# A feed-forward in seven block products instead of eight, in an encoder layer on one core

## The chip, the core and the metric

The kernel runs on one core of a Trainium2 chip. Five engines work side by side, each through its own instructions in order: TensorE (PE in the profile, its weight loads PEld), VectorE (DVE), ScalarE (ACT), GpSimd (POOL) and SyncE (SP, which issues the transfers here). Data lie in device memory, in SBUF (128 partitions) and in PSUM (eight banks of 128 x 512 floats, into which TensorE adds up). The metric is the device time of one execution in microseconds (us), the median of the runs.

## The reference

One layer of a hybrid encoder is applied to two request groups of 512 tokens, with the same weights, in float32. With D = 1024 and a feed-forward width of 2816, cut to what matters here:

```python
h = rmsnorm(x, g_mix)
u = h @ w_in                      # feeds an mLSTM, an attention and merge gates
...
x = x + (g_m * y_m + g_a * y_a) @ w_out     # y_m = (sigmoid(o) * hm) @ w_mo, y_a = attention @ w_ao

h2 = rmsnorm(x, g_ffn)
x = x + (silu(h2 @ w_gate) * (h2 @ w_up)) @ w_down

x = x + sigmoid(x @ w_ple_gate) * (p_l @ w_ple)
return rmsnorm(x, g_final)        # after the only layer
```

## The kernel before, in words

**Tiles.** Activations are held transposed: a tile has 128 features on the partitions and the 512 tokens of one group along the row. So `x` is eight tiles per group (`KD` = 8), and the feed-forward's inner activations are 22 (`NF`). The two groups are `g` = 0 and 1.

**Precision.** Every operand of a product is split into a high part (`hi`, type fp32r, a cast on ACT) and the rest (`lo`, a subtraction on DVE, `lo_of`). A product is three matmuls: hi by hi, hi by lo and lo by hi. `proj1` does that for one column block of 128 outputs: for each of eight slices of the contraction three matmuls into one bank, 24 in all.

**Weights.** `weight(src)` loads a column block of a weight (128 x 1024) into a staging tile `wst`, makes `whi` on ACT and `wlo` on DVE; `w8(name)` picks the block from a table. There are two buffers of each, so the next block's weights are made while TensorE works. Each block serves both groups: 48 matmuls.

**Order of the stages.** Input and first norm; gates and four mLSTM heads with their projections; attention over eight heads with merge gates between; then the part that the change touches: the mLSTM's output projection (`mo`, with values `z1` kept in SBUF), the attention's (`ao`, which makes `y`), the output projection (`out`, which adds the residual into `x2`), the feed-forward, the embedding stage, and the final norm of each group.

**Feed-forward before.** The operands `h2` are `x2` times the gain `g_ffn`, split, without the rows' norm: they are made while the output projection still runs. The norm `rs2` of each group is applied to the products afterwards. The 22 inner column blocks come in three parts (`FF_PARTS` = 8, 8, 6). In a part, for each inner block the gate product is scaled by the norm, put through Silu and scaled again, then multiplied with the up product, and split; then eight `w_down` blocks (`wd0` to `wd2`) are multiplied with the part's activations and added to `x2`.

**Embedding stage before.** `x2` is split again (`x3`). For each of eight column blocks and both groups there are a gate product (`pg`, 24 matmuls) and a product of the embedding's projection (`emb`: `wple` by `pp`, six matmuls), then `embed` on ACT and DVE. The second group's last four blocks come after the first group's, whose final norm is computed meanwhile; its last two blocks run in halves of 256 tokens.

**What sets the order.** A planner orders each engine's instructions when the kernel is built: it takes the written order as priority, gives out buffer slots as they come free, and places the waits. Two stages can thus mix on an engine. A pool of tiles (`Slots`) gives each tag a fixed number of slots; pools opened after others are closed reuse their memory, and their tiles wait for the old ones that they overlap.

Of the kernel before, what the change touches and what calls it, by code (L numbers as in the profile page):

```python
# [62 lines left out]
def encoder_kernel(ctx: ExitStack, tc: tile.TileContext, a):  # L63
# [3 lines left out]
    cp = ctx.enter_context(tc.tile_pool(name="const", bufs=1))  # L67
    wp = ctx.enter_context(tc.tile_pool(name="wp", bufs=1))
    sm = ctx.enter_context(tc.tile_pool(name="sm", bufs=1))
# [4 lines left out]
    def nm(s):  # L74
        ids[0] += 1
        return f"{s}_{ids[0]}"

    class Slots:
# [8 lines left out]
        def close(self):  # L87
            self.ctx.close()

    EV = Slots("EV", ch=2, bk=2)  # L90

# [50 lines left out]
    def weight(src):  # L142
        n = src.shape[-1]
        st = wp.tile([P, 1024], F32, name=nm("wst"), tag="wst", bufs=WB[0])
        nc.sync.dma_start(st[:, :n], src)
        hi = wp.tile([P, 1024], F32R, name=nm("whi"), tag="whi", bufs=WB[1])
        S.copy(hi[:, :n], st[:, :n])  # L147
        lo = wp.tile([P, 1024], F32R, name=nm("wlo"), tag="wlo", bufs=WB[2])
        lo_of(lo[:, :n], st[:, :n], hi[:, :n])
        return hi, lo  # L150
# [12 lines left out]
    def w8(name):  # L163
        return weight(a["w8"][W8[name]])
# [82 lines left out]

    # ---- input, scaled by the first gain; its rows' norms are applied to the products
    LAT = Slots("LAT", raw=8)
# [49 lines left out]

    # ---- gate rows, compressed q and kv  # L300
    gsd = [dr.tile([64, T], F32, name=f"gsd{g}") for g in range(G)]
# [16 lines left out]

    # ---- gates
    nmr = MC.pool.tile([P, T], F32R, name="nmr")  # L320
# [102 lines left out]

    # ---- mLSTM heads
    R.close()
# [146 lines left out]

    # ---- norms of the compressed q and kv, on top of their rows' first norm
    def lat_norms():
# [186 lines left out]
    z1 = [[None] * KD for _ in range(G)]  # L761
# [14 lines left out]
    for c in range(KD):  # L776
        w = w8(f"ao{c}")
        for g in range(G):
            bk = proj1(w, ox[g])
            t = load(tad[g][c])  # L780
            V.scalar_tensor_tensor(out=t, in0=t, scalar=1.0, in1=bk, op0=ALU.add, op1=ALU.mult)
            V.tensor_tensor(out=t, in0=t, in1=z1[g][c], op=ALU.add)
# [4 lines left out]
            y[g][c] = (hi, lo)  # L787

    # ---- output projection, residual, second norm
    x2 = [[None] * KD for _ in range(G)]  # L790
    h2 = [[None] * KD for _ in range(G)]
    ss = [SumSq(L, "tr") for _ in range(G)]
    for c in range(KD):
        w = w8(f"out{c}")
        for g in range(G):
            bk = proj1(w, y[g])
            x = load(a[f"x{g}"][c], QL, "lat", "x2")
            V.tensor_tensor(out=x, in0=x, in1=bk, op=ALU.add)
            x2[g][c] = x
            ss[g].add(x)  # L800
            h2[g][c] = gsplit(x, col("g_ffn", c), L, "B", "h2")
    rs2 = []
    for g in range(G):
        t = H("rs", "rs2")
        S.copy(t, ss[g].rstd_bank(D))
        rs2.append(t)

    # ---- feed-forward
    f0 = 0
    for pi, nf in enumerate(FF_PARTS):  # L810
        act = [[], []]
        for f in range(f0, f0 + nf):
            w = w8(f"fg{f}")
            sg = []
            for g in range(G):
                s = L("tr", "sg")
                V.tensor_tensor(out=s, in0=rs2[g], in1=proj1(w, h2[g]), op=ALU.mult)  # L817
                S.activation(out=s, in_=s, func=AF.Silu)
                V.tensor_tensor(out=s, in0=s, in1=rs2[g], op=ALU.mult)
                sg.append(s)  # L820
            w = w8(f"fu{f}")
            for g in range(G):
                V.tensor_tensor(out=sg[g], in0=sg[g], in1=proj1(w, h2[g]), op=ALU.mult)  # L823
                act[g].append(split(sg[g], H, "h", "ac"))
        for c in range(KD):
            w = weight(a[f"wd{pi}"][c])
            for g in range(G):
                V.tensor_tensor(out=x2[g][c], in0=x2[g][c], in1=proj1(w, act[g], nf), op=ALU.add)  # L828
        f0 += nf

    # ---- per-layer embedding; the second group ends after the first, which is normed meanwhile
    def final_norm(g, b0=0, nb=NB, pool=(2, 5)):
        tok, n = slice(b0 * P, (b0 + nb) * P), nb * P
        bc = ss[g].rstd_bank(D, b0, nb)
        rf = H("rs", "rsf")[:, tok]
        S.copy(rf, bc)
        per = T // n
        for c0 in range(0, KD, per):
            ob = H("h", "o")
            for i in range(per):  # L840
                c = c0 + i
                o, x = ob[:, i * n : (i + 1) * n], x2[g][c][:, tok]
                if c in pool:
                    S.activation(out=o, in_=x, func=AF.Copy, scale=col("g_final", c))
                    GP.tensor_tensor(out=o, in0=o, in1=rf, op=ALU.mult)
# [7 lines left out]
    pp = [[split(load(a[f"p{g}"][k]), H, "h", "pl") for k in range(2)] for g in range(G)]  # L853
    x3 = [[None] * KD for _ in range(G)]
    for c in range(KD):
        for g in range(G):
            x3[g][c] = split(x2[g][c], L, "B", "x3")
    wple = []
    for i in range(2):
        st = wp.tile([P, 1024], F32, name=nm("wst"), tag="wst", bufs=WB[0])  # L860
        nc.sync.dma_start(st, a["wple"][i])
        for j in range(2):
            wple.append(split(st[:, j * T : (j + 1) * T], H, "h", "we"))
    ss = [SumSq(L, "tr") for _ in range(G)]

    def embed(c, g, bp, bk, tok=slice(0, T)):
        t, x = EV("ch", "pt")[:, tok], x2[g][c][:, tok]
        S.activation(out=t, in_=bk, func=AF.Tanh, scale=0.5)
        V.scalar_tensor_tensor(out=t, in0=t, scalar=1.0, in1=bp, op0=ALU.add, op1=ALU.mult)
# [3 lines left out]
    def emb(c, g, tok=slice(0, T)):  # L873
        return proj1(wple[c // 2], pp[g], 2, (c % 2) * 256, tok=tok)

    lead = KD - LAG
    for c in range(lead):
        w = w8(f"pg{c}")
        bks = [proj1(w, x3[g]) for g in range(G)]
        for g in range(G):  # L880
            embed(c, g, emb(c, g), bks[g])
    for c in range(lead, KD):
        bk = proj1(w8(f"pg{c}"), x3[0])
        embed(c, 0, emb(c, 0), bk)
    ws = [w8(f"pg{c}") for c in range(lead, lead + 2)]
    final_norm(0)
    for c in range(lead, KD - 2):
        bk = proj1(ws.pop(0), x3[1])
        ws.append(w8(f"pg{c + 2}"))
        embed(c, 1, emb(c, 1), bk)  # L890
    for b0, nb in ((0, NB // 2), (NB // 2, NB // 2)):
        tok = slice(b0 * P, (b0 + nb) * P)
        for c in range(KD - 2, KD):
            bp = emb(c, 1, tok)
            embed(c, 1, bp, proj1(ws[c - KD + 2], x3[1], tok=tok), tok)
        final_norm(1, b0, nb, (2, 5) if b0 else range(KD))
    L.close()
    QL.close()
    H.close()
    LAT.close()  # L900
    EV.close()
    banks(None, None)


WB = (2, 2, 2)
LAG = 4
# [95 lines left out]
```

## Time and profile before

| | |
|---|---|
| median of 3 runs | 2009.96 us (2009.62 to 2010.03) |
| span of the profiled execution, first to last instruction | 2009.2 us; no other time is listed for that execution |
| mean granted TensorE clock | 0.994 |
| busy in the span | PE 1980.5, DVE 983.7, ACT 691.7, POOL 67.7 us |
| transfers | 140.93 MB, mean 70 GB/s |

Busy time of PE counts overlapping matmuls once in the totals; a single matmul's duration is longer than the distance to the next one, so the rate is read from how many start in a window. The wait lists say which engine waited for which; an entry under SPq is a transfer that waits in SyncE's queue before it is issued. POOL's spans are rough.

### The profile page before, as it was taken

To read this page: it belongs to the slowest core of one execution; us is meant where nothing else is said; L and a number is where in the kernel's file an instruction comes from. 1 tells how busy PE (TensorE), PEld (TensorE's weight loads), DVE (VectorE), ACT (ScalarE), POOL (GpSimd) and SP (SyncE) were. 2 spreads that over 40 slices of the span, in tenths; PEclk is the share of its full clock that TensorE was granted. 3 is DMA by queue.
4 is the path that set the end of the run, shared out by engine and by line. 5 is a ranking of instruction groups with operands and counts; after the bars stand their busy time and mean duration, and the time that the engine had idled before them with its cause. 6 is when DMAs were issued, how large, how long until landed. Compare 5 with 4: busy or idle time off the path is not lost.

```text
span 2009.2 us, 23492 instructions
## 1 busy us (share of the span) xinstructions
PE 1980.5 (99%) x9318; PEld 1627.7 (81%) x9318; DVE 983.7 (49%) x1799; ACT 691.7 (34%) x1303; POOL 67.7 (3%) x88
## 2 busy tenths in 40 slices
PE   7999999999999999999999999999999999999996
PEld 6788898988888787888888888888888888888886
DVE  6747575745554767843444533322333222334436
ACT  5345455525344657841122321211121101212223
POOL 3000000000000000000000000000000000000002
PEclk9999999999999999999999999999999999999998
DMA  4110101111341212532431111111111111111212
GB/s 155 48 43 32 64 33 53 38 68 69 118 155 66 90 44 91 190 130 74 137 126 53 43 43 52 43 53 42 53 43 53 42 53 42 53 35 61 74 53 95
DMA packets 62734, 140.93 MB, mean 70 GB/s; under 512 B 6752, under 2 KB 17376, under 8 KB 62624
## 3 DMA queue, kind: packets, MB, share of 16 engines
q1 hardware_dynamic: 62624, 139.43, 20.0%
q8 instruction: 73, 1.20, 0.2%
q14 instruction: 37, 0.30, 0.0%
HBM read 113.88 MB, written 25.53 MB: 69 GB/s over the span
## 4 chain that ended last, share of the span: by engine, by line
PE 97%; DVE 2%; ACT 1%; issue 0%; DMA 0%; DVEq 0%; SPq 0%; ACTq 0%
PE mm L160 26%; PE mm L158 26%; PE mm L159 26%; PE nm L546 3%; PE mm L464 2%; PE mm L463 2%; PE mm L465 2%; PE pt L722 1%; PE pj L158 1%; PE pj L159 1%; PE pj L160 1%; PE sc L705 1%; PE av L729 1%; PE av L731 1%; PE av L730 1%; PE sc L709 1%
## 5 line engine op out<-in xcount | busy, mean ns | idle before, releaser
L147 ACT CAST whi<-wst 128x1024 fp32r<-128x1024 f32 (+1 forms) x159 | 163.9, 1031 | 556.7 <-PE mm L159 500.5
L160 PE MATMUL mm<-h2h,wlo 128*128 128x512 f32 x704 | 279.2, 397 | 0.0
L158 PE MATMUL mm<-h2h,whi 128*128 128x512 f32 x704 | 279.1, 396 | 0.0
L159 PE MATMUL mm<-h2l,whi 128*128 128x512 f32 x704 | 279.1, 396 | 0.0
L158 PE MATMUL mm<-hh,whi 128*128 128x512 f32 x592 | 237.1, 401 | 7.0 <-ACT whi L147 6.8
L160 PE MATMUL mm<-hh,wlo 128*128 128x512 f32 x592 | 236.2, 401 | 2.3 <-DVE wlo L133 2.2
L159 PE MATMUL mm<-hl,whi 128*128 128x512 f32 x592 | 237.0, 401 | 1.1 <-DVE hl L245 1.1
L133 DVE TENSOR_TENSOR wlo<-wst,whi 128x1024 fp32r<-128x1024 f32 (+1 forms) x159 | 191.6, 1205 | 90.1 <-ACT whi L147 89.6
L159 PEld LDWEIGHTS mm<-h2l,whi 128*128 128x128 f32 x704 | 132.6, 188 | 32.3
L160 PEld LDWEIGHTS mm<-h2h,wlo 128*128 128x128 f32 x704 | 132.6, 188 | 32.3
L158 PEld LDWEIGHTS mm<-h2h,whi 128*128 128x128 f32 x704 | 132.6, 188 | 32.2
L158 PEld LDWEIGHTS mm<-hh,whi 128*128 128x128 f32 x592 | 113.0, 191 | 33.4 <-ACT whi L147 6.8
L160 PE MATMUL mm<-ach,wlo 128*128 128x512 f32 x352 | 139.6, 396 | 0.0
L159 PE MATMUL mm<-acl,whi 128*128 128x512 f32 x352 | 139.6, 396 | 0.0
L158 PE MATMUL mm<-ach,whi 128*128 128x512 f32 x352 | 139.5, 396 | 0.0
L160 PEld LDWEIGHTS mm<-hh,wlo 128*128 128x128 f32 x592 | 112.6, 190 | 29.2 <-DVE wlo L133 3.4
L159 PEld LDWEIGHTS mm<-hl,whi 128*128 128x128 f32 x592 | 112.8, 191 | 28.6 <-DVE hl L245 2.3
L828 DVE TENSOR_TENSOR x<-x,mm 128x512 f32<-128x512 f32 x48 | 33.0, 687 | 159.9 <-PE mm L160 159.9
L823 DVE TENSOR_TENSOR sg<-sg,mm 128x512 f32<-128x512 f32 x44 | 30.2, 688 | 140.2 <-PE mm L160 140.2
L817 DVE TENSOR_TENSOR sg<-rs,mm 128x512 f32<-128x512 f32 x44 | 30.3, 688 | 138.3 <-PE mm L160 136.6
L158 PEld LDWEIGHTS mm<-ach,whi 128*128 128x128 f32 x352 | 66.3, 188 | 16.2
L159 PEld LDWEIGHTS mm<-acl,whi 128*128 128x128 f32 x352 | 66.3, 188 | 16.2
(289 smaller groups left out, 3700.5 us busy)
## 6 DMA issues: line engine op xcount, KB each, us to landing
wst<-w SPq DMA_DIRECT2D x125, 512.0 KB
x<-x SPq DMA_DIRECT2D x32, 256.0 KB
wst<-wd SPq DMA_DIRECT2D x16, 512.0 KB
hzd<-hz SPq DMA_DIRECT2D x16, 256.0 KB
tmd<-tg SPq DMA_DIRECT2D x16, 256.0 KB
tad<-tg SPq DMA_DIRECT2D x16, 256.0 KB
vd<-av SPq DMA_DIRECT2D x16, 256.0 KB
avt<-vd SPq DMA_DIRECT2D x16, 256.0 KB
```

The source lines that it names most:

```text
L133: e.tensor_tensor(out=out, in0=src, in1=hi.bitcast(F32), op=ALU.subtract)
L147: S.copy(hi[:, :n], st[:, :n])
L158: E.matmul(bk, whi[:, c], hi, start=k == 0, stop=False)
L159: E.matmul(bk, whi[:, c], lo, start=False, stop=False)
L160: E.matmul(bk, wlo[:, c], hi, start=False, stop=k == nk - 1)
L463: E.matmul(out, hi[:, tb], whi[:, n], start=k == 0, stop=False)
L464: E.matmul(out, lo[:, tb], whi[:, n], start=False, stop=False)
L465: E.matmul(out, hi[:, tb], wlo[:, n], start=False, stop=k == KD - 1)
L546: E.matmul(bk, l, r, start=n == 0, stop=n == len(terms) - 1)
L817: V.tensor_tensor(out=s, in0=rs2[g], in1=proj1(w, h2[g]), op=ALU.mult)
L823: V.tensor_tensor(out=sg[g], in0=sg[g], in1=proj1(w, h2[g]), op=ALU.mult)
L828: V.tensor_tensor(out=x2[g][c], in0=x2[g][c], in1=proj1(w, act[g], nf), op=ALU.add)
```

## The change

The feed-forward's products are regrouped as 2 x 2 blocks in the manner of Strassen (in Winograd's form). The three pairs are: two halves of the contraction; two column blocks of the weight, `f1` and `f2` (or `c` and `c + 1`); and the two request groups. Where eight block products would be written, seven are made, from sums and differences of weight blocks and of operand blocks, and their results are added in PSUM or on the way out.

- **Weights.** `Seven` holds two staged column blocks as four quarters a11, a12, a21, a22. `weights(name)` makes the quarter or sum that a product needs (four sums per block, on POOL), then its `hi` and `lo`.
- **Operands.** `h2` is now seven sets of four tiles, made from `x2` times gain times norm, so that the norm comes first. Sums are on POOL, splits on ACT and DVE. They fill 56 of the 64 slots `op`.
- **Order of the products.** `run` interleaves two blocks: while the current one does P6, P5, Q4 and P3, the next does P1, P2 and P7 in between. P6, P5 and P3 add onto the bank of P1 (`b1`) after it has been read, Q4 onto that of P7 (`b2`).
- **Results.** For gate and up, `outputs` copies a bank on ACT and adds or subtracts another on DVE. The activations' products and their four differences are made on POOL mostly and stored to device memory (`actd`, seven tiles per pair). The down runs load them back, split them, and add or subtract the banks into `x2`.
- **All gate and up blocks come first, then the three down parts,** instead of part by part.
- **Embedding.** Its projections are computed between the output projection and the feed-forward, copied out by ACT and stored (`emd`); `embed` loads them back. Their operands are loaded and split before the output projection.
- **Memory.** `z1` goes to device memory and back. `x2` lies in a pool of its own (`X2`), and the pools of weights, operands and banks are opened anew for the feed-forward (`W`, `OP`, `PF`). Weight tiles there are 512 wide, five of each kind; the embedding stage's gate weights are made in halves (`halves`, `proj2`).

The core of the diff:

```diff
-            z1[g][c] = t
+            nc.sync.dma_start(z1d[g][c], t)
...
-            h2[g][c] = gsplit(x, col("g_ffn", c), L, "B", "h2")
-    rs2 = []
-    for g in range(G):
-        t = H("rs", "rs2")
-        S.copy(t, ss[g].rstd_bank(D))
-        rs2.append(t)
+    rs2 = [ss[g].rstd_bank(D) for g in range(G)]
+    for c in range(KD):
+        for g in range(G):
+            t = EV(("ch", "bk")[g], "em")
+            S.copy(t, proj1(wple[c // 2], pp[g], 2, (c % 2) * 256))
+            nc.sync.dma_start(emd[g][c], t)
...
+    W = Slots("W", wst=4, s3=2, wh=5, wl=5)
+    OP = Slots("OP", op=OPS, ev=8)
...
+        def weights(self, name):
+            n, (a11, a12, a21, a22) = self.n, self.st
+            if name == "P1":
+                src = a11
+            elif name == "P2":
+                src = a12
+            elif name == "P7":
+                src = W("s3", "s3")[:, :n]
+                GP.tensor_tensor(out=src, in0=a11, in1=a21, op=ALU.add)
+                GP.tensor_tensor(out=a21, in0=a21, in1=a22, op=ALU.add)
+            elif name == "P6":
+                GP.tensor_tensor(out=a11, in0=a11, in1=a21, op=ALU.add)
+                src = a11
+            elif name == "P5":
+                src = a21
+            elif name == "Q4":
+                src = a22
+            else:
+                GP.tensor_tensor(out=a12, in0=a12, in1=a11, op=ALU.add)
+                src = a12
+            hi = W("wh", "wh", F32R)[:, :n]
+            S.copy(hi, src)
+            lo = W("wl", "wl", F32R)[:, :n]
+            lo_of(lo, src, hi)
+            return hi, lo
...
+            for k in range(self.kh):
+                c = slice(k * P, (k + 1) * P)
+                hi, lo = self.ops[name][k]
+                E.matmul(bk, whi[:, c], hi, start=bool(first) and k == 0, stop=False, **sk)
+                E.matmul(bk, whi[:, c], lo, start=False, stop=False, **sk)
+                E.matmul(bk, wlo[:, c], hi, start=False, stop=k == self.kh - 1, **sk)
+            self.out(name, self.bk)
...
+    def run(makers):
+        cur, nxt = None, makers[0]()
+        for n in ("P1", "P2", "P7"):
+            nxt.product(n)
+        for i in range(len(makers)):
+            cur, nxt = nxt, makers[i + 1]() if i + 1 < len(makers) else None
+            for n in ("P6", "+P1", "P5", "+P2", "Q4", "+P7", "P3"):
+                if n[0] != "+":
+                    cur.product(n)
+                elif nxt:
+                    nxt.product(n[1:])
...
+    for k in range(KD // 2):
+        t = {}
+        for n, g, kk in (("a", 0, k), ("c", 0, k + 4), ("b", 1, k), ("d", 1, k + 4)):
+            t[n] = OP("op", "hn")
+            V.scalar_tensor_tensor(
+                out=t[n], in0=x2[g][kk], scalar=col("g_ffn", kk), in1=rs2[g], op0=ALU.mult, op1=ALU.mult
+            )
+        for n in ("P1", "P2", "P7", "P6", "P5", "Q4", "P3"):
...             (P1 takes a, P2 takes c, P3 takes d; t3, t2, t1 and t4 are differences and sums on POOL)
+            h2[n].append(split_op(t[n]))
...
+            if name in ("P1", "P6", "P5"):
+                t = OP("ev", "u")
+                S.copy(t, bk["b1"])
+                keep[name] = t
+            if name in ("P2", "P5", "Q4"):
+                t = keep[{"P2": "P1", "P5": "P5", "Q4": "P6"}[name]]
+                b = bk["b0" if name == "P2" else "b2"]
+                V.tensor_tensor(out=t, in0=b, in1=t, op=ALU.add if name == "P2" else ALU.subtract)
...
+        for n in NAMES:
+            for j in range(nf // 2):
+                ops[n].append(split_op(load(actd[f0 + j, n], OP, "ev")))
...
+                elif name == "P5":
+                    put(x2[1][c2], bk["b1"], ALU.subtract)
+                    put(x2[1][c2], bk["b2"])
```

More of the change, by code (lines that the diff above doesn't have):

```diff
@@ L88, in close @@
             self.ctx.close()
+    WP = Slots("WP", wst=2, whi=2, wlo=2)
     EV = Slots("EV", ch=2, bk=2)
@@ L760, in encoder_kernel @@
             hx[g][k] = gsplit(load(hzd[g][k], QL, "lat"), hg[:, k : k + 1], H, "h", "hm")
[L761 removed]
+    z1d = [[dr.tile([P, T], F32, name=f"z1d{g}_{c}") for c in range(KD)] for g in range(G)]
     for c in range(KD):
@@ L787, in encoder_kernel @@
             y[g][c] = (hi, lo)
+    L.close()
+    QL.close()
+    X2 = Slots("X2", "right", x=16)
+    O = Slots("O", tr=4, pl=16)
     x2 = [[None] * KD for _ in range(G)]
-    h2 = [[None] * KD for _ in range(G)]
-    ss = [SumSq(L, "tr") for _ in range(G)]
+    pp = [[split(load(a[f"p{g}"][k], O, "tr"), O, "pl", "pl") for k in range(2)] for g in range(G)]
+    wple = []
+    for i in range(2):
+        st = WP("wst", "wst", F32, (P, 1024))
+        nc.sync.dma_start(st, a["wple"][i])
+        for j in range(2):
+            wple.append(split(st[:, j * T : (j + 1) * T], O, "pl", "we"))
+    ss = [SumSq(O, "tr") for _ in range(G)]
     for c in range(KD):
@@ new lines, in encoder_kernel, with split_op, __init__, product @@
+    O.close()
+    H.close()
+    LAT.close()
+    EV.close()
+    WP.close()
+    W = Slots("W", wst=4, s3=2, wh=5, wl=5)
+    OP = Slots("OP", op=OPS, ev=8)
+    def split_op(src):
+        return split(src, OP, "op", "x")
+    class Seven:
+        def __init__(self, srcs, kh, ops, out):
+            n = kh * P
+            st = []
+            for src in srcs:
+                t = W("wst", "wst", F32, (P, 1024))
+                nc.sync.dma_start(t[:, : 2 * n], src)
+                st += [t[:, 0:n], t[:, n : 2 * n]]
+            self.st, self.n, self.kh, self.ops, self.out = st, n, kh, ops, out
+            self.bk = {}
+        def weights(self, name):
[23 more added lines that the diff above has]
+            return hi, lo
+        def product(self, name):
+            whi, wlo = self.weights(name)
+            b, first = {"P1": ("b1", 1), "P6": ("b1", 0), "P5": ("b1", 0), "P3": ("b1", 0), "P2": ("b0", 1),
+                        "P7": ("b2", 1), "Q4": ("b2", 0)}[name]
+            if first:
+                self.bk[b] = bank(b)
+            bk = self.bk[b]
+            sk = dict(skip_group_check=True)
+            for k in range(self.kh):
[5 more added lines that the diff above has]
+            self.out(name, self.bk)
@@ new lines, in gate_up, with gate, up, make @@
+    def gate_up(f1, f2):
+        sg, ac = {}, {}
+        def gate(at, t):
+            sg[at] = OP("op", "sg")
+            S.activation(out=sg[at], in_=t, func=AF.Silu)
+        def up(at, t):
+            e = V if at == (0, 1) else GP
+            e.tensor_tensor(out=sg[at], in0=sg[at], in1=t, op=ALU.mult)
+            ac[at] = sg[at]
+            if len(ac) == 4:
+                a_, b_, c_, d_ = (ac[x] for x in ((0, 0), (0, 1), (1, 0), (1, 1)))
+                t1, t3, t2, t4 = (OP("ev", "t") for _ in range(4))
+                GP.tensor_tensor(out=t1, in0=a_, in1=b_, op=ALU.subtract)
+                GP.tensor_tensor(out=t3, in0=b_, in1=d_, op=ALU.subtract)
+                GP.tensor_tensor(out=t2, in0=t3, in1=a_, op=ALU.subtract)
+                GP.tensor_tensor(out=t4, in0=t2, in1=c_, op=ALU.add)
+                for n, t_ in zip(NAMES, (a_, c_, t3, t2, t1, t4, d_)):
+                    actd[f1, n] = dr.tile([P, T], F32, name=nm("actd"))
+                    nc.sync.dma_start(actd[f1, n], t_)
+        def make(kind, put):
+            return lambda: Seven([a["w8"][W8[f"{kind}{f}"]] for f in (f1, f2)], 4, h2, outputs(put))
+        return [make("fg", gate), make("fu", up)]
@@ L825, in encoder_kernel, with halves @@
[L825 to L828, printed above, removed]
-        f0 += nf
+        run(down(pi, f0, nf))
+        f0 += nf
+    banks("P4", dict(mm=5, tp=1, bc=2), mm="mm", tp="ssc", bc="rbc")
+    def halves(src):
+        st = W("wst", "wst", F32, (P, 1024))
+        nc.sync.dma_start(st, src)
+        out = []
+        for j in range(2):
+            hi = W("wh", "wh", F32R)
+            S.copy(hi, st[:, j * T : (j + 1) * T])
+            lo = W("wl", "wl", F32R)
+            lo_of(lo, st[:, j * T : (j + 1) * T], hi)
+            out.append((hi, lo))
+        return out
@@ new lines, in proj2, with __call__ @@
+    def proj2(ws, x, tok=slice(0, T)):
+        bk = bank()[:, tok]
+        for k in range(KD):
+            whi, wlo = ws[k // 4]
+            c = slice(k % 4 * P, k % 4 * P + P)
+            hi, lo = (v[:, tok] for v in x[k])
+            E.matmul(bk, whi[:, c], hi, start=k == 0, stop=False)
+            E.matmul(bk, whi[:, c], lo, start=False, stop=False)
+            E.matmul(bk, wlo[:, c], hi, start=False, stop=k == KD - 1)
+        return bk
+    class Sl:
+        def __call__(self, tag, n, dt=F32, shape=(P, T)):
+            return OP("ev" if tag == "ch" else "op", n, dt, shape)
```

139 lines of the change are left out of this document (84 added, 55 removed).

## The prediction, made before the changed kernel had run

> **What bounds the kernel now.** I read the page first (shares, slices, chain), then a table of windows over the stages, then groups by shape, waits, and short timelines.
>
> ```profile
> span 2009.2 us, 23492 instructions
> ...
> PE 1980.5 (99%) x9318; PEld 1627.7 (81%) x9318; DVE 983.7 (49%) x1799; ACT 691.7 (34%) x1303; POOL 67.7 (3%) x88
> ...
> POOL 3000000000000000000000000000000000000002
> PEclk9999999999999999999999999999999999999998
> ...
> PE 97%; DVE 2%; ACT 1%; issue 0%; DMA 0%; DVEq 0%; SPq 0%; ACTq 0%
> ```
>
> TensorE holds 97% of the chain that ended last, at full clock; POOL does nothing in the slices of the feed-forward. The windows are the output projection, the feed-forward, the embedding stage and the tail:
>
> ```profile
> core 0: us, PE busy (x) PEld busy (x) DVE busy (x) ACT busy (x) POOL busy (x), PEclk, DMA share, GB/s
> 1041.90:1131.60 89.70, 89.70 (x384) 72.14 (x383) 40.61 (x54) 27.38 (x39) 0.00 (x0) 1.00 0.15 53
> 1131.60:1876.70 745.10, 745.10 (x3190) 599.40 (x3190) 252.95 (x345) 138.15 (x184) 0.00 (x0) 1.00 0.14 48
> 1876.70:1990.60 113.90, 113.90 (x555) 94.87 (x553) 54.72 (x90) 34.84 (x56) 3.10 (x2) 1.00 0.18 65
> ```
>
> TensorE has no gap in any of the three. The output projection is the cleanest ruler: 384 matmuls of 512 columns in 89.70 us, 0.2336 us each. The durations in the next rows (397 ns) overlap; the pitch is what counts.
>
> ```profile
> L160 PE MATMUL mm<-h2h,wlo 128*128 128x512 f32 x704 | 279.2, 397 | 0.0
> L160 PE MATMUL mm<-ach,wlo 128*128 128x512 f32 x352 | 139.6, 396 | 0.0
> ```
>
> Each row is one of three terms, so the feed-forward has 3 x (704 + 352) = 3168 matmuls; 3168 x 0.2336 = 740 us, which agrees with the window of 745.1 (it also holds the norm's small matmuls).
>
> **The change, part by part.**
>
> Matmuls. The new blocks: 22 for gate and up (two column blocks, 4 slices per half), 8 in the first two down parts (4 slices) and 4 in the last (3 slices). Seven products of 4 x 3 = 12 matmuls make 84, or 63 with 3 slices: 30 x 84 + 4 x 63 = 2772. Removed: 396 x 0.2336 = 92.5 us. One product now lasts 2.80 us (2.10 with 3 slices), one block 19.6 us. Nothing adds matmuls; the 96 of the embedding (22.4 us) only move ahead. This is on the path in full: span 2009.2 - 92.5 = 1916.7 us before new stalls.
>
> Engines beside it. Rows that price the added work:
>
> ```profile
> L133 DVE TENSOR_TENSOR wlo<-wst,whi 128x1024 fp32r<-128x1024 f32 x143 | 176.3, 1233 | 77.2 <-ACT whi L147 76.8
> L828 DVE TENSOR_TENSOR x<-x,mm 128x512 f32<-128x512 f32 x48 | 33.0, 687 | 159.9 <-PE mm L160 159.9
> L133 POOL TENSOR_TENSOR vnl<-avt,vnh 128x512 fp32r<-128x512 f32 x16 | 21.1, 1317 | 363.9 <-ACT vnh L137 219.7 <-DVE knl L133 121.0 <-DMA ozd<-oz 23.2
> L818 ACT ACTIVATE sg<-sg 128x512 f32<-128x512 f32 x44 | 27.7, 630 | 106.3 <-DVE sg L817 106.2
> L137 ACT CAST x3h<-x 128x512 fp32r<-128x512 f32 x16 | 9.9, 621 | 26.3 <-DVE x L828 25.8
> L245 DVE SCALAR_TENSOR_TENSOR h2l<-x,cols,h2h 128x512 fp32r<-128x512 f32 x16 | 12.0, 750 | 1.4 <-ACT h2h L243 1.4
> L133 DVE TENSOR_TENSOR x3l<-x,x3h 128x512 fp32r<-128x512 f32 x16 | 11.0, 689 | 5.5 <-ACT x3h L137 5.5
> L643 ACT COPY av<-mm 128x512 f32<-128x512 f32 x16 | 9.4, 586 | 11.2 <-PE mm L641 9.2 <-DMA vd<-av 1.2 <-ACT qnh L137 0.4
> ```
>
> Per block: ACT 7 weight casts, 3 bank copies and (gate) 4 Silu: 14 x 0.62 = 8.7 us. DVE 7 low halves x 0.689 + 3 bank operations x 0.687 (one more for up) = 6.9 to 7.6 us. POOL 4 weight sums, for up also 3 multiplies and 4 differences. In a gate/up pair: ACT 15, DVE 14.5, POOL 15 x 1.317 = 19.8 us, under TensorE's 39.2. So no engine alone becomes the bound. But POOL and DVE delay each other:
>
> ```profile
> 12.87 1.29 POOL L268 TENSOR_TENSOR x<-x,x 128x512 f32<-128x512 f32 x1 [1.96 <-ACT x L266]
> 21.69 2.02 POOL L264 TENSOR_TENSOR x<-x 128x512 f32<-128x512 f32 x1 [4.42 <-DVE hl L245]
> ...
> 20.87 0.74 DVE L245 SCALAR_TENSOR_TENSOR hl<-x,cols,hh 128x512 fp32r<-128x512 f32 x1
> 22.73 1.52 DVE L245 SCALAR_TENSOR_TENSOR hl<-x,cols,hh 128x512 fp32r<-128x512 f32 x1
> ...
> 1989.37 0.17 DVE L175 TENSOR_SCALAR ri<-rv 128x4 int32<-128x4 int32 x1
> 1995.44 0.65 DVE L175 TENSOR_SCALAR ri<-rv 128x4 int32<-128x4 int32 x1
> ...
> 1993.98 5.48 POOL L845 TENSOR_TENSOR o<-o,rsf 128x256 f32<-128x256 f32 x8 [11.32 <-ACT rsf L836]
> ```
>
> The same DVE operation takes 0.74 us, and 1.52 us when it starts inside POOL's 2.02; a four-column one goes from 0.17 to 0.65 while POOL issues one operation per 5.48/8 = 0.69 us. So they take turns. Counted as one shared queue, a pair needs 15 x 1.29 + 14 x 0.689 = 29.0 us of 39.2: full to 74%, not over. The Trainium skill, GPSIMD Engine Reference, Specifications, says that GpSimd shares its SBUF interfaces with VectorE and names operations with two SBUF inputs as those in conflict; every low half here is one. The trace agrees. Its section Performance versus the Vector engine, which puts GpSimd at about half of VectorE's pace on such sums, speaks against putting 11 of them in an up block; by it alone the sum would not change, as POOL stays under 39.2.
>
> Weights. A cast and a low half per product instead of one of each per 48 matmuls; five slots of each let them run four products, 11 us, ahead, against 0.62 + 0.689 + at most 2.02 for a POOL operation in the way: hidden. The load for the block after next starts when P3's low half frees its staging tile, some 8 us into a block's 19.6; its first product starts at 22.4. That leaves 14 us, and even at the 48 GB/s of the feed-forward's window half a megabyte takes 11. For now these loads wait for slots, not the slots for loads:
>
> ```profile
> SPq L145 <- DVE wlo L133: 1157.4, 132, 23.5
> PE mm L158 <- ACT whi L147: 6.8, 1, 6.8
> ```
>
> The 6.8 us is the kernel's start; TensorE waits nowhere later for a weight's cast. Behind SP's new stores (77 operand tiles of 256 KB, and 77 loads back in the down runs) weight loads can queue: I take 0; 11 us if each up block's seven stores hold one up for 1 us more than its margin.
>
> Bank hand-offs. The products accumulate onto banks that are read in between: Q4 may start only when P5's bank was copied (ACT) and subtracted (DVE), with one product of the next block, 2.80 us, as cover. With a weight cast and low half ahead in the queues: 0.62 - 0.23 + 0.586, then 0.687, and 0.3 for signals = 1.96 us: hidden; with a low half caught behind POOL up to 0.62 - 0.23 + 1.29 + 0.689 + 0.687 + 0.3 = 3.4 us: 0.6 us late. Down with 3 slices has two 0.687 additions against 2.10 us. I take a stall of 0.2 us in 30 blocks: 6 us (ends 0 and 0.6 x 34 = 20).
>
> Run ends. There are four (gate/up, three down); the last block has no successor between its products, so P6 to P5 and P5 to Q4 lie open, 1.2 + 2.0 us each time unless the next run's first product fills in, its operands needing slots of the old ones. Ends 0 and 4 x 3.2 = 13; I take 4, since the order of issue already mixes stages (small norm matmuls sit among the products).
>
> Entry into the feed-forward, the largest unknown. Before, the products ran on un-normed operands, with the norm applied afterwards. Now seven operand sets need the norm first: 16 scaled tiles (DVE 0.750), 16 sums on POOL, 28 splits (ACT 0.621, DVE 0.689): DVE 16 x 0.750 + 28 x 0.689 = 31.3 us, POOL 16 x 1.29 = 20.6. The norms of before:
>
> ```profile
> 1132.07 0.69 DVE L798 TENSOR_TENSOR x<-x,mm 128x512 f32<-128x512 f32 x1 [2.81 <-PE mm L160]
> ...
> 1138.11 0.68 DVE L209 TENSOR_TENSOR diag<-ident,rl 128x512 fp32r<-128x512 f32 x1
> ...
> 1143.45 0.68 DVE L209 TENSOR_TENSOR diag<-ident,rl 128x512 fp32r<-128x512 f32 x1
> ```
>
> From the end of the output projection, group 0's is ready after 6.8 us, group 1's after 12. In the written order the last slice of P1's operand is about the 36th of 44 DVE operations. With three done early, it is ready at 12 + 33 x 0.71 = 35.5 us, or 51 us if twelve POOL sums take their turns in between. TensorE's cover is the moved embedding's 22.4 us, norm matmuls 2, and three of four slices of P1 and P2, 4.2 us: 28.6. The stall is 7 to 22 us. It is 0 if group 0's operands, all that P1 and P2 need, are issued first (16 operations from 6.8 us: ready at 18); 40 if preparation ran wholly in series (12 + 31.3 + 20.6 - 24.4). I take 14, the middle of the inner pair. An idle TensorE also restarts slowly:
>
> ```profile
> 18.41 0.80 PE L160 MATMUL mm<-hh,wlo 128*128 128x512 f32 x1 [2.22 <-DVE wlo L133]
> ...
> 18.40:23.70 5.30, 5.29 (x13) 4.13 (x13) 5.30 (x8) 4.13 (x7) 2.01 (x2) 0.50 0.32 106
> ```
>
> After a 2.22 us wait at the start, 13 matmuls took 5.3 us at a clock of 0.50, against 13 x 0.2336 = 3.0: 2 us more. Entry: 16 us. The Trainium skill, TensorE: Matmul & The Clock Gate, Part 1, puts the half rate down to an idle window of about 3.4 us; by it short hand-off stalls cost no clock, which is how I count them.
>
> The moved embedding. Its 4 + 2 loads and 8 splits (ACT 5.0, DVE 5.5 us) now pass SP's, ACT's and DVE's queues beside the output projection, where DVE is busy 40.6 of 89.7 us and loses 16 splits of 0.75 us: 0. If the loads hold up the residual's, five banks (28 us of products) stand between that and TensorE. Its 16 bank copies (ACT 9.4 us) and stores fall into the entry beside 28 casts (17.4 us): 27 us of ACT, less than DVE's 31.3 there. The 16 loads back in the last stage replace products; late, they would hold DVE's additions, with five banks ahead again.
>
> Tail and rest, together. Moving the embedding also takes 5.6 us of TensorE cover (4 x 6 x 0.2336) from group 0's final norm, which ends 6 us before the last matmul: +1 (0 to 3). Half-width matmuls cost half a pitch, so their removal is worth nothing. The values z1 go through memory now, 32 transfers of 256 KB around two projections, and the next one moves 53 GB/s: 0; late ones would delay DVE's sums, behind TensorE's banks.
>
> Sum: 1916.7 + 16 + 6 + 4 + 1 = 1943.7 us of span. The runs' median, 2009.96, is 0.8 above the span: 1944.
>
> **The rivals.**
>
> *All hidden.* Group 0 first, hand-offs within 2.80 us, run ends filled: 1916.7 + 0.8 = 1917.5, to 1930 with part of it. For it: no TensorE gap in 948 us of windows now. Against: DVE and POOL are nearly idle there now, and will not be at the entry.
>
> *Hand-offs late in every block.* If the DVE's in-order queue regularly holds a low half behind POOL ahead of the subtraction: 0.6 to 1.1 us in 34 blocks, and the entry's 22 instead of 14: 1944 - 6 + 30 + 8 = 1976. Against: POOL is half empty in gate and down.
>
> *Slower: the shared port saturates in gate/up.* At the slowest durations seen, 15 x 2.02 + 14 x 1.52 = 51.6 us per pair against 39.2: 12.4 x 11 = 136 us, 2080. It turns the change into a loss from (2010 - 1944)/11 = 6 us per pair, 45 us. Against: the 2.02 and the 1.52 contain each other's wait, so they count one turn twice.
>
> **How the numbers follow.** Forecast (1930 to 1958) 0.46; all hidden 0.22; hand-offs late (1958 to 1985) 0.20; a mixture up to 2005 0.07; port saturated 0.05. The range 1919 to 1980 leaves out the slow cases and the corners of the two nearest ones. Less than 0.2% (4 us) would not be told from no change: faster 0.94, same 0.01, slower 0.05.
>
> **What would show it.** About 8900 TensorE matmuls; a feed-forward of about 670 us with the entry's gap; POOL busy some 370 us (68 now, and 229 operations x 1.317 more); a TensorE gap of 10 to 20 us after the embedding's products, ended by a DVE split, followed by a half-clock stretch; short waits of the Q4 products on a DVE subtraction. Wrong if TensorE waits for weight low halves behind POOL all through gate/up, or if the entry's gap is absent.

## The result, and the profile after

The changed kernel takes 1965.9 us (median; 1964.3 to 1968.0) against 2009.8 (2008.3 to 2010.0) before: ratio 0.978, 95% interval 0.9767 to 0.9794. The prediction was 1944, range 1919 to 1980. The page of the profile after, with the lines that answer to those of before:

```profile
span 1962.5 us, 24424 instructions
...
PE 1855.5 (95%) x8910; PEld 1554.5 (79%) x8910; DVE 1148.9 (59%) x2023; ACT 831.8 (42%) x1610; POOL 408.3 (21%) x317
...
POOL 3000000000000001000000044565566472323002
PEclk9999999999999999999999978999999999999996
...
PE 88%; DVE 6%; DMA 2%; ACT 2%; issue 1%; POOL 1%; SPq 0%; DVEq 0%; ACTq 0%; POOLq 0%
```

TensorE runs 408 matmuls fewer (9318 to 8910: the 396, and 12 because the embedding's last products are no longer cut in halves), GpSimd 229 operations more. TensorE's share of the chain fell from 97% to 88%, and two slices of the clock, at the start of the feed-forward, fell. The windows of the changed kernel are the mLSTM's and the attention's output projections, the output projection, the entry into the feed-forward, its steady part, the passage from gate/up to down, and the tail:

```profile
core 0: us, PE busy (x) PEld busy (x) DVE busy (x) ACT busy (x) POOL busy (x), PEclk, DMA share, GB/s
817.00:1023.10 206.10, 206.10 (x934) 170.56 (x932) 100.39 (x163) 70.32 (x117) 2.97 (x2) 1.00 0.51 169
1036.45:1125.00 88.55, 88.55 (x384) 73.22 (x385) 28.62 (x36) 16.47 (x22) 0.00 (x0) 0.98 0.11 36
1149.60:1200.00 50.40, 14.18 (x37) 9.02 (x37) 42.00 (x43) 18.48 (x32) 31.91 (x19) 0.56 0.14 52
1200.00:1600.00 400.00, 400.00 (x1765) 331.10 (x1764) 188.16 (x225) 150.71 (x259) 230.84 (x155) 1.00 0.30 104
1600.00:1700.00 100.00, 87.03 (x367) 70.41 (x366) 74.00 (x108) 49.91 (x86) 34.63 (x23) 0.95 0.61 204
1927.80:1962.50 34.70, 4.12 (x15) 3.11 (x13) 19.04 (x53) 9.24 (x23) 7.97 (x10) 0.54 0.28 97
```

The same windows of the kernel before, for the first and the last row:

```profile
830.00:1041.90 211.90, 211.90 (x934) 171.24 (x933) 101.25 (x164) 70.96 (x118) 2.97 (x2) 1.00 0.41 139
1990.60:2009.20 18.60, 2.80 (x10) 1.88 (x8) 11.77 (x31) 2.57 (x7) 7.36 (x10) 0.58 0.34 113
```

Two things stand there that the prediction did not have. First, the same 934 matmuls take 5.8 us less, at full clock, in a stage where the change left the arithmetic alone; and that stage begins 13 us earlier (817.0 in place of 830.0) although nothing ahead of it computes anything else. In the steady part of the feed-forward a matmul follows every 400/1765 = 0.2266 us; the ruler of the prediction was 0.2336. Second, TensorE waits far more than predicted. TensorE's waits after:

```profile
PE b L885 <- ACT xh L137: 34.3, 4, 10.5
PE mm L158 <- ACT whi L147: 20.2, 2, 13.3
PE ssc L196 <- DVE sq L234: 17.8, 2, 9.0
PE b L885 <- ACT wh L869: 9.5, 2, 5.7
```

The whole difference, at 0.2266 us per matmul: -92.5 for the removed products (at the old pitch). For the shorter pitch -13 ahead of 817, -5.8 in this window, -2.7 in the output projection, 2772 x 0.0070 = -19.4 in the feed-forward and some -3 behind it: -44. For stalls +15 ahead of the output projection (13.3 and 2 of half clock), +42 at the entry (50.4 less 37 matmuls), +17 at the passage to down (100 less 367 matmuls), +1 at later run ends, +16 in the tail (34.7 in place of 18.6): 91. Together -45.5; the two spans differ by -46.7 (1962.5 less 2009.2). So the stalls gave back what the removed products saved, and what is left is about the size of the shorter pitch.

Where the stalls come from, in the changed kernel's timeline. Ahead of the output projection:

```profile
1004.01 0.33 SPq L799 DMA_DIRECT2D wst<-wple  x1
...
1025.17 2.16 ACT L137 CAST plh<-ld 128x512 fp32r<-128x512 f32 x4
1027.24 2.17 ACT L137 CAST weh<-wst 128x512 fp32r<-128x512 f32 x4
...
1029.63 1.53 SPq L145 DMA_DIRECT2D wst<-w  x2
...
1036.42 0.79 PE L158 MATMUL mm<-yh,whi 128*128 128x512 f32 x1 [13.27 <-ACT whi L147]
```

Both staging tiles `wst` are given to the embedding's weight by 1004, but its casts run only at 1027. In ScalarE's queue they stand behind the casts of `p`, whose tiles (pool `O`) lie on memory that the attention projection uses to its end, at 1023. Only then can the output projection's first weight be loaded. At the entry:

```profile
1128.12 22.67 SPq L819 DMA_DIRECT2D emd<-em  x16
1150.90 1.80 SPq L843 DMA_DIRECT2D wst<-w  x4
...
1136.39 1.40 DVE L908 SCALAR_TENSOR_TENSOR hn<-x,cols,rbc 128x512 f32<-128x512 f32 x2
...
1149.86 0.59 ACT L818 COPY em<-mm 128x512 f32<-128x512 f32 x1 [0.77 <-PE mm L160]
1150.35 1.14 ACT L137 CAST xh<-hn 128x512 fp32r<-128x512 f32 x2
...
1151.00 1.30 DVE L133 TENSOR_TENSOR xl<-hn,xh 128x512 fp32r<-128x512 f32 x2 [7.70 <-ACT xh L137]
...
1155.45 0.79 PE L885 MATMUL b<-xh,wh 128*128 128x512 f32 x1 [5.67 <-ACT wh L869]
1164.77 0.79 PE L885 MATMUL b<-xh,wh 128*128 128x512 f32 x1 [7.67 <-ACT xh L137]
...
1180.06 0.80 PE L885 MATMUL b<-xh,wh 128*128 128x512 f32 x1 [10.48 <-ACT xh L137]
...
1191.68 1.22 PE L885 MATMUL b<-xh,wh 128*128 128x512 f32 x2 [8.47 <-ACT xh L137]
```

The first weights are loaded behind the 16 stores of the embedding (`emd`). The first two normed tiles are made by 1137.8, but their casts `xh` stand in ScalarE's queue behind the last of the embedding's 16 copies (`em`), and so the first operands are split only when its products have ended. Then TensorE waits 7.7 to 10.5 us for each further slice of the contraction. At the passage to down, and in the tail:

```profile
1616.55 0.32 SPq L969 DMA_DIRECT2D actd<-sg  x1
1616.92 2.34 SPq L754 DMA_DIRECT2D ld<-actd  x5
...
1620.32 1.22 PE L885 MATMUL b<-xh,wh 128*128 128x512 f32 x2 [7.67 <-ACT xh L137]
1642.55 0.50 PE L885 MATMUL b<-xh,wh 128*128 128x512 f32 x1 [3.80 <-ACT wh L869]
...
1921.32 0.59 ACT L1058 COPY rsf<-rbc 128x512 f32<-128x512 f32 x1 [8.35 <-PE rbc L215]
...
1923.04 0.59 ACT L1084 ACTIVATE pt<-mm 128x512 f32<-128x512 f32 x1
...
1937.11 0.98 PE L196 MATMUL ssc<-onesr,sq 128*128 128x2 f32 x4 [9.00 <-DVE sq L234]
```

The loads of the down operands stand in SyncE's queue behind the last pair's stores. In the tail ScalarE idles 8.35 us for group 0's norm (`rsf`) with group 1's `pt` queued behind it, and TensorE waits twice for `sq`, 17.8 us in all.

### The profile page after: what moved, and what is told of

Read it like the earlier page. It is cut to its first block, busy times and chain, and to the rows that moved or that the text cites. A ratio compares the mean times of both kernels' runs of the same rounds, so it can differ in the third digit from the quotient of the medians.

```text
span 1962.5 us, 24424 instructions
## 1 busy us (share of the span) xinstructions
PE 1855.5 (95%) x8910; PEld 1554.5 (79%) x8910; DVE 1148.9 (59%) x2023; ACT 831.8 (42%) x1610; POOL 408.3 (21%) x317
## 4 chain that ended last, share of the span: by engine, by line
PE 88%; DVE 6%; DMA 2%; ACT 2%; issue 1%; POOL 1%; SPq 0%; DVEq 0%; ACTq 0%; POOLq 0%
PE mm L158 11%; PE mm L160 11%; PE mm L159 11%; PE b L885 10%; PE b L887 10%; PE b L886 10%; PE nm L546 3%; PE mm L463 2%; PE mm L465 2%; PE mm L464 2%; PE mm L1042 1%; PE mm L1043 1%; PE mm L1041 1%; PE pt L722 1%; DVE xl L133 1%
## 5 line engine op out<-in xcount | busy, mean ns | idle before, releaser
L885 PE MATMUL b<-xh,wh 128*128 128x512 f32 x924 | 358.9, 394 | 46.1 <-ACT xh L137 34.3
L886 PE MATMUL b<-xl,wh 128*128 128x512 f32 x924 | 362.6, 392 | 3.9 <-DVE xl L133 3.9
L887 PE MATMUL b<-xh,wl 128*128 128x512 f32 x924 | 358.8, 392 | 0.0
L133 DVE TENSOR_TENSOR wl<-wst,wh 128x512 fp32r<-128x512 f32 (+1 forms) x228 | 205.1, 901 | 153.7 <-ACT wh L869 132.6
L869 ACT CAST wh<-wst 128x512 fp32r<-128x512 f32 (+1 forms) x204 | 124.0, 609 | 284.3 <-PE b L886 248.1
L885 PEld LDWEIGHTS b<-xh,wh 128*128 128x128 f32 x924 | 175.0, 190 | 87.0 <-ACT xh L137 36.8
L886 PEld LDWEIGHTS b<-xl,wh 128*128 128x128 f32 x924 | 175.0, 189 | 41.5 <-DVE xl L133 5.2
L887 PEld LDWEIGHTS b<-xh,wl 128*128 128x128 f32 x924 | 175.0, 189 | 36.5 <-DVE wl L133 0.2
L147 ACT CAST whi<-wst 128x1024 fp32r<-128x1024 f32 (+1 forms) x79 | 81.5, 1031 | 149.1 <-PE mm L159 125.1
L133 DVE TENSOR_TENSOR wlo<-wst,whi 128x1024 fp32r<-128x1024 f32 (+1 forms) x79 | 95.8, 1212 | 34.2 <-ACT whi L147 33.7
```

The source lines that it names most:

```text
L133: e.tensor_tensor(out=out, in0=src, in1=hi.bitcast(F32), op=ALU.subtract)
L869: S.copy(hi, src)
L885: E.matmul(bk, whi[:, c], hi, start=bool(first) and k == 0, stop=False, **sk)
L886: E.matmul(bk, whi[:, c], lo, start=False, stop=False, **sk)
L887: E.matmul(bk, wlo[:, c], hi, start=False, stop=k == self.kh - 1, **sk)
```

## The experiments

Each ratio is to the kernel before, run beside it. That kernel's median lay between 2009.8 and 2011.5 us in these, so times from different rows of the table can be compared to about 2 us.

| run | us | ratio (95%) |
|---|---|---|
| changed kernel | 1965.9 | 0.9780 (0.9767 to 0.9794) |
| e1, before with the weights' pool moved | 1961.2 | 0.9759 (0.9744 to 0.9773) |
| e3, operands put out of step | 1983.4 | 0.9868 (0.9852 to 0.9885) |
| e4, embedding's loads later | 1967.8 | 0.9790 (0.9776 to 0.9805) |
| e10, staging tiles of their own | 1949.1 | 0.9696 (0.9681 to 0.9710) |
| e6, operands product by product | 1956.9 | 0.9736 (0.9721 to 0.9750) |
| e9, sums on VectorE | 1958.6 | 0.9746 (0.9729 to 0.9764) |
| e5, embedding back | 1952.5 | 0.9706 (0.9690 to 0.9722) |
| e8, down loads from ScalarE | 1960.4 | 0.9750 (0.9736 to 0.9765) |
| e7, order of the tail | 1956.9 | 0.9732 (0.9718 to 0.9747) |
| c1, edits together, embedding ahead | 1918.2 | 0.9537 (0.9521 to 0.9553) |
| c2, edits together, embedding back | 1927.2 | 0.9587 (0.9573 to 0.9601) |
| c3, c1 with all norms first | 1919.5 | 0.9540 (0.9524 to 0.9556) |

**The pitch: e1 and e3.** In the program before, the weight tiles start on multiples of 64 bytes and the operand tiles 32 bytes off one; the changed kernel opens the weights' pool behind the small constants, and both are 32 off.

```diff
-    wp = ctx.enter_context(tc.tile_pool(name="wp", bufs=1))
     sm = ctx.enter_context(tc.tile_pool(name="sm", bufs=1))
+    wp = ctx.enter_context(tc.tile_pool(name="wp", bufs=1))
```

> The kernel before, with one line moved: the pool of the weight tiles is opened behind the small-constants pool, so that the weight tiles lie 32 bytes off a multiple of 64, as the operands do (before: weights on a multiple of 64, operands 32 off it). Instructions and their order are unchanged. Address theory: the distance from one 512-column matmul to the next falls from 234 to 227 ns in every product with a staged weight, as it is in the changed kernel from its start: 13.0 us up to the mLSTM's output projection, 5.9 in the next two projections, 2.9 in the output projection, 3168 x 7.6 ns = 24 in the feed-forward, 3 in the embedding stage: 49 us, about 1961. Then the changed kernel, at 1966, owes its gain to this and the seven products with their stalls come to about nothing. Rival, that the shorter pitch belongs to the chip or to the execution or to the new instructions: 2010, pitch 234.

Measured 1961.2, as the address theory had it. The output projection of this kernel:

```profile
1017.40:1104.40 87.00, 87.00 (x385) 72.06 (x384) 39.93 (x54) 27.30 (x40) 0.00 (x0) 1.00 0.18 61
```

385 matmuls in 87.0 us, 0.226 each, with the instructions of before in the order of before. One moved line is worth as much as the whole change: the changed kernel stands at 0.9780, this one at 0.9759, and the intervals overlap.

```diff
     W = Slots("W", wst=4, s3=2, wh=5, wl=5)
+    PD = Slots("PD", pad=1)
+    PD("pad", "pad", F32, (P, 8))
     OP = Slots("OP", op=OPS, ev=8)
```

> The changed kernel with a 32-byte pad between the feed-forward's weight pool and its operand pool: weights stay 32 bytes off a multiple of 64, operands move onto one; all else as it is, and nothing moves before the feed-forward. Theory, that what counts is the offset between weight and operand tile: the pitch stays 227 ns up to the feed-forward and is 234 in it and in the embedding stage: 2772 + 384 matmuls x 7.6 ns = +24 us, about 1990. Rival, that only weight tiles on a multiple of 64 are slow: pitch 227 throughout, 1966.

Measured 1983.4, +17.5 us. Ahead of the feed-forward nothing changes, and in it the pitch is 400/1716 = 0.2331:

```profile
1210.00:1610.00 400.00, 400.00 (x1716) 321.32 (x1715) 186.26 (x215) 141.92 (x246) 224.36 (x153) 1.00 0.28 101
```

Weights off and operands on a multiple of 64 is slow, as the reverse is before; both off is fast. So the rival of e3 is out, and where the tiles start is the cause. Two rules fit all of this: that the two must have the same offset, or that neither may start on a multiple of 64. Both on a multiple would tell them apart and was not run. The trace of the kernel before already holds both paces: between matmuls whose tiles both start 32 bytes off, in the attention above all, the median distance is 227 ns and the mean 229 (326 distances), and with the weights on a multiple both are 234 (6293 distances). That the time rose by 17.5 and not 24 fits 3156 x (0.2331 - 0.2266) = 20.5, with some of it in time that TensorE waited anyway.

**The stall ahead of the output projection: e4 and e10.** e4 calls the embedding's loads and splits ahead of the fourth output block.

> The changed kernel with the loads and splits of the embedding's operands (p and its weight) moved from ahead of the output projection to ahead of its fourth block. Theory: the wait of 13.3 us ahead of the output projection (the two embedding weights hold both staging tiles until the attention projection's memory is free) goes, with some 2 us of half clock behind it: about 1951. Rival, that it only moves: the splits then come late for the embedding's products or the residual's loads, and the time is 1960 to 1966.

Measured 1967.8: the rival. TensorE runs into the output projection without a stall, and stands 15.68 us for `whi` at 1070 instead: the loads still took both staging tiles early (SyncE issued them at 1025 and 1035), and the casts came later.

```profile
1070.66 0.79 PE L158 MATMUL mm<-yh,whi 128*128 128x512 f32 x1 [15.68 <-ACT whi L147]
```

e10 leaves the place and changes the tiles:

```diff
-        st = WP("wst", "wst", F32, (P, 1024))
-        nc.sync.dma_start(st, a["wple"][i])
         for j in range(2):
-            wple.append(split(st[:, j * T : (j + 1) * T], O, "pl", "we"))
+            wple.append(split(load(a["wple"][i][:, j * T : (j + 1) * T], O, "tr"), O, "pl", "we"))
```

> The changed kernel with the embedding weight's four half tiles loaded into staging tiles of their own pool (the pool O's, as p's) in place of the two staging tiles that all weights share. Theory, that the 13.3 us ahead of the output projection are those two staging tiles, held until the attention projection's memory is free (in the run that moved the loads to the fourth block a stall of 16 us stood there instead): the stall goes and does not come back, about 1951. Rival, that any place for these loads ahead of the feed-forward costs the same: 1963 to 1968.

Measured 1949.1; the output projection and the end of the stage before it run through:

```profile
1012.00:1110.00 98.00, 98.00 (x434) 81.16 (x433) 39.64 (x54) 23.63 (x34) 0.00 (x0) 1.00 0.30 102
```

That was expected. So the shared staging tiles were the cause, worth 16.8 us.

**The entry: e6, e9 and e5.** e6 turns the two loops of the operands around, so that all four slices of a product's operand are made before the next product's.

> The changed kernel with the feed-forward's operands made product by product (all four slices of P1, then of P2, and so on) in place of slice by slice. Theory, that the entry's stall is the order: P1 then needs four normed tiles and four splits of group 0 alone; of the 42 us lost between 1149.6 and 1200 some 17 stay (the first weights' wait of 5.7 us and POOL's sums for P7): about 1941 (1935 to 1950). Rival, that the entry is bound by what VectorE and GpSimd have to do in turns, with operand memory that is free only when the embedding's products end: the same work stands behind 1150, the gain is under 10 us: 1956 to 1966.

Measured 1956.9, 9.0 us less: the rival's figure. In the window of the entry (50.4 us from the end of the embedding's products) 74 matmuls run in place of 37, so 33.6 us are lost in place of 42:

```profile
1149.60:1200.00 50.40, 27.21 (x74) 18.31 (x74) 47.23 (x45) 19.89 (x35) 40.56 (x24) 0.70 0.19 65
```

e9 leaves the order and gives the 16 sums to VectorE.

> The changed kernel with the 16 sums and differences of the normed feed-forward input on VectorE in place of GpSimd. Theory, that VectorE and GpSimd take turns at the entry (a low half takes 1.70 us there, 0.69 alone): a slice needs 4 x 0.75 + 7 x 0.69 + 4 x 0.69 = 10.6 us of VectorE in place of the 12 to 15 us that it takes now, so 8 to 16 us less, about 1954. Rival, that VectorE's own work is the limit and GpSimd's runs beside it: 16 x 0.69 = 11 us more, about 1977.

Measured 1958.6, 7.3 us less and just short of the 8 to 16 that were expected: 58 matmuls in 50.1 us, 37 lost. The turns are to be seen in this run: the same three low halves, first beside GpSimd's weight sums and then without GpSimd.

```profile
1157.08 5.10 DVE L133 TENSOR_TENSOR xl<-t,xh 128x512 fp32r<-128x512 f32 x3
...
1174.56 1.88 DVE L133 TENSOR_TENSOR xl<-t,xh 128x512 fp32r<-128x512 f32 x3
```

```profile
1158.37 1.59 POOL L857 TENSOR_TENSOR wst<-wst 128x512 f32<-128x512 f32 x1
1160.04 1.59 POOL L859 TENSOR_TENSOR wst<-wst,wst 128x512 f32<-128x512 f32 x1
1161.59 1.71 POOL L856 TENSOR_TENSOR s<-wst,wst 128x512 f32<-128x512 f32 x1
```

1.70 us each against 0.63, with one GpSimd operation of 1.6 to 1.7 us between two of them. This agrees with the Trainium skill, GPSIMD Engine Reference, Specifications, on the SBUF interfaces that GpSimd shares with VectorE. e5 undoes the move of the embedding.

> The changed kernel with one part undone: the embedding's projections are computed in the last stage again, beside the gate products, and nothing of them is loaded, split or stored before. Theory, that moving them ahead costs more than it covers: the stall ahead of the output projection goes (13.3 us and 2 of half clock) and the tail is 16 us shorter; at the entry the products' 22 us of cover go, but the operand slots are free earlier and no stores stand ahead of the first weight loads, so the loss there grows from 42 us to some 51: -22 us, about 1944. Rival, that the cover at the entry is worth its full 22 us: 1966 - 15 - 1 + 22 = 1972.

Measured 1952.5, 13 us less than the changed kernel: the move is a loss as it was made, though less of one than expected. TensorE starts the first product there 16.6 us after the last matmul of the output projection (1126.32 against 1109.77), with nothing of the embedding in between; then it goes slice by slice as before, at 11.6 us each:

```profile
1126.32 0.79 PE L871 MATMUL b<-xh,wh 128*128 128x512 f32 x1 [1.72 <-ACT xh L137]
...
1137.94 0.79 PE L871 MATMUL b<-xh,wh 128*128 128x512 f32 x1 [8.47 <-ACT xh L137]
...
1149.56 0.80 PE L871 MATMUL b<-xh,wh 128*128 128x512 f32 x1 [8.47 <-ACT xh L137]
```

**The passage to down: e8.** `split_op(load(actd[...], OP, "ev"))` issues its load from ScalarE's queue.

> The changed kernel with the down runs' 77 operand loads issued from ScalarE's queue in place of SyncE's. Theory, that the 17 us lost between gate/up and down come from the issue (the loads stand in SyncE's queue behind the last pair's stores until 1616.9): they start up to 10 us earlier, about 1958. Rival, that the transfers themselves are the limit (28 tiles of 262 KB at the 351 GB/s seen there are 21 us, and their slots come free only with the last gate/up block): under 3 us, 1963 to 1969.

Measured 1960.4, between the two. 387 matmuls run from 1600 to 1700, in place of 367: 12.3 us lost in place of 16.8, so the issue was about a third of it. The first load starts only 3.3 us earlier, at 1613.61, and not up to 10.

```profile
1600.00:1700.00 100.00, 91.61 (x387) 73.98 (x386) 79.45 (x112) 51.07 (x87) 39.01 (x26) 0.95 0.64 216
```

The wait of 7.67 us for the next operand is still 6.55. That the rest is the transfers' rate was not tried; for it speaks that the DMA engines of the changed kernel are full from 1620 to 1630 (share 1.01, 351 GB/s).

**The tail: e7.** Group 0's final norm and the halves of group 1 are written behind the last products.

> The changed kernel with the written order of the last stage changed: group 0's final norm and group 1's first half come after the last products of group 1 have been worked in. Theory, that the tail's extra 16 us (last product to end 34.7 us, 18.7 before) are VectorE's and ScalarE's queues, in which a norm that waits for TensorE stands ahead of the work on group 1's last products: 10 to 14 us less, about 1954. Rival, that the chain of the second group itself is as long: 1963 to 1968.

Measured 1956.9, 9.0 us less where 10 to 14 were expected. From the last product to the end it is 28.6 us in place of 34.7; the wait of 9.0 us for `sq` is 0.26 to 0.88. What stands there now is one wait:

```profile
1938.15 1.87 PE L215 MATMUL rbc<-diag,onesr 128*128 128x256 f32 x4 [7.18 <-DVE diag L209]
```

**The edits together: c1, c2, c3.**

> The changed kernel with the embedding ahead of the feed-forward as it is, and the single edits put together: its weights through staging tiles of their own (-15), operands made product by product with the sums on VectorE (-9 and -7 apart), the last stage's order (-9), down operands loaded from ScalarE's queue (-5.5); also the embedding's products group by group and their stores from ScalarE's queue, so that the first weight loads do not stand behind them (the 5.7 us wait). If the edits add up: 1966 - 15 - 16 - 9 - 5.5 - 4 = 1916. Rival, that the two entry edits overlap and the entry stays bound by memory that is free only after the embedding's products: 1928 to 1935.

> The kernel with the embedding's products back in the last stage (1952.5), with operands made product by product and the sums on VectorE, the last stage's order, and down operands loaded from ScalarE's queue. If the entry shrinks as group 0's operands can be split as soon as its norm is there (first product some 8 us after the output projection, VectorE's 47 us of work against 27 us of products behind it): 1952.5 - 18 - 5.5 - 4 = 1925. Rival, that without the embedding's products as cover the entry keeps its loss: 1938 to 1943.

Measured 1918.2 and 1927.2: the edits add up. Apart, the five of c1 gained 16.8, 9.0, 7.3, 9.0 and 5.5 us, 47.6 in all; together they gained 47.7. The sixth, which takes the embedding's stores off SyncE's queue, was not run apart; with it the first weights of the feed-forward are loaded at 1129.11, 7 us before the embedding's products end. The entry window of c1, as long as those above:

```profile
1136.20:1186.60 50.40, 34.83 (x120) 26.25 (x120) 47.86 (x70) 28.70 (x50) 37.83 (x12) 0.80 0.16 57
```

120 matmuls in place of 37, 23 us lost. With the entry and the staging mended, the embedding ahead is the better place after all, by 9 us (c1 against c2). c3 writes all 16 normed tiles ahead of the first split.

> The combined kernel with the embedding ahead (1918.2), with all 16 normed tiles of the feed-forward's input written ahead of the first split. There VectorE makes four of them at 1123 to 1126 and then idles 12.75 us for ScalarE's first operand cast, which waits for the embedding's last products and copies. Theory, that the other twelve (12 x 0.69 = 8.2 us) fit into that idle time: 6 to 8 us less, about 1911. Rival, that their slots too lie on memory that the embedding's operands hold, or that the entry's gaps are set by the weight sums on GpSimd (a wait of 4.35 us for one at 1149): 1916 to 1920.

Measured 1919.5: no gain. Ten tiles are made at once, then VectorE waits until the embedding's products end:

```profile
1122.66 6.91 DVE L908 SCALAR_TENSOR_TENSOR hn<-x,cols,rbc 128x512 f32<-128x512 f32 x10
1135.41 4.04 DVE L908 SCALAR_TENSOR_TENSOR hn<-x,cols,rbc 128x512 f32<-128x512 f32 x6 [5.85 <-PE mm L160]
```

Memory is a limit, as the rival had it, but not the one that decides: all 16 tiles were there by 1139.5, and the time was the same. What then sets the rest was not separated further.

Against e1, which has the same offset with eight products, c1 is 43 us faster. That is what the regrouping, with the moves around it, brought here of the 396 x 0.2266 = 89.7 that the seven products save. In c1 the entry still loses 23 us, and its tail is longer than that of the kernel before (28 us in place of 18.6).

## Why the prediction was right in the time and wrong in its parts

The time lay 22 us above the forecast and inside the range, by two large errors of opposite sign. That is luck: with the slow pitch in the feed-forward and the last stage alone, the same kernel took 1983.4 (e3), outside the range of 1919 to 1980.

- **Matmuls, -92.5: right.** 8910 were named as about 8900.
- **The pitch of 0.2336, taken for all: the step that failed first.** It was read from the cleanest window and held constant. The change moved a pool, the pitch became 0.2266, and that gave 44 us (49 in e1). The diff showed the moved pool; the prediction did not mention it, and the faster matmuls were there to be seen in the attention of the kernel before.
- **Entry, 16 with ends 0 and 40: mis-sized, 42.** The sign named for it (a gap of 10 to 20 us ended by a VectorE split, then half clock) came as six gaps of 1.1 to 10.5 us, most of them ended by ScalarE, with a clock of 0.56 over the window. The last slice of P1's operand, put at 35.5 or 51 us behind the output projection, was multiplied at 66.7 (1191.68 less 1125.0). Three steps failed. The norms were read as ready at their `diag` rows, 6.8 and 12 us, but a matmul and its wait follow: in the kernel before, group 0's norm was copied at 12.3 us, and in the changed kernel the first tile that uses it starts at 11.4 (1136.39).

```profile
1143.89 0.59 ACT L805 COPY rs<-rbc 128x512 f32<-128x512 f32 x1 [9.80 <-PE rbc L215]
```

The preparation was then counted from the norms, but the first low half was made only at 1151: the casts stood behind the embedding's copies in ScalarE's queue. Later tiles also wait for operand slots on the embedding's memory, as c3 shows. Which of the two costs more was not separated. And the first weights, taken as hidden, queued behind the embedding's stores. The turns with GpSimd, which the prediction had priced at the entry, are real (e9). The rival of late hand-offs lay near in time (1976), but its mechanism did not occur.

- **The moved embedding, 0: wrong, 15.** The prediction looked at the residual's loads and five banks. The price was in two staging tiles (e10).
- **Bank hand-offs, 6: too much.** None in 400 us of the steady part. Nor did GpSimd hold anything up there, though its operations took (408.3 - 67.7)/229 = 1.49 us in place of 1.29 to 1.317; the rival of the saturated port did not occur.
- **Run ends, 4: mis-sized, 18.** 17 of it at the first down run, where loads stood behind stores (a third, e8); the cause of the rest is open. "The order of issue already mixes stages" held at the later ones: 1.3 us in two waits.
- **Tail, +1: wrong, 16.** Counted was the cover of TensorE, not that a norm that waits for it heads two queues. Writing that norm and group 1's halves later took back 6 us of the tail (e7); the chain behind the last product that is left, with its wait of 7.18 us, was not looked into.
- **Weights hidden, and z1 at 0: right in the steady part.** The stage with z1 shows no gap in 206 us. In the feed-forward weights were waited for twice, 5.67 us at the entry and 3.80 at the first down run.
- **Signs.** The feed-forward was named at about 670 us and took 689 (1149.6 to 1838.9), GpSimd's busy time at 370 and was 408.

## What to carry to other kernels

Take a regrouping's saving as a bound and list, for each queue, memory region and staging tile that a moved step shares, what it holds up: four stalls here gave back nearly the whole saving, and each went or shrank with a small edit. When a diff moves an allocation, compare the matmul pitch in stages that it leaves alone before crediting the arithmetic. Undoing one part can mislead while another fault stands: the moved embedding lost 13 us until the staging and the entry were mended, and won 9 afterwards.

## What the runs showed of the hardware that was not expected

Matmuls of 512 columns (fp32r) follow every 0.2266 us when weight and operand tile both start 32 bytes off a multiple of 64, and every 0.2331 to 0.2336 when one of them starts on a multiple and the other 32 off, whichever it is. Other offsets were not run, nor both on a multiple, so whether the offset between the two counts or the multiple itself is open. The Trainium skill, TensorE: Matmul & The Clock Gate, Part 1, gives a column a cycle at 2.4 GHz and about 2.5 ns more, 215.7 ns for 512 columns; the steady window here, 400 us at a granted clock of 1.00, shows 226.6.
